# Ten instead of four gate blocks by seven products, six instead of twelve as filler work, and three smaller edits in the attention stage

## The chip, the cores and the metric

One core of a Trainium2 chip runs the kernel. The core has a matrix engine (TensorE, PE in the profile, its weight loads PEld), a vector engine (VectorE, DVE), a scalar engine (ScalarE, ACT), a general engine (GpSimd, POOL) and SyncE (SP), which here issues all DMA transfers. Each engine works its own list of instructions in order, and semaphores make it wait for others. The metric is the device time of one execution in microseconds; lower is better.

## The reference

The input is x, 1024 tokens by 1024 channels, float32. One layer is computed:

```
h = x @ w_in                                   # 1024 x 5120
qa, ka, va, qb, kb, vb, ga, gb = split(h)      # 3 x 512, 3 x 512, 1024, 1024 columns
y_a = chunk_band_attention(qa, ka, va, rel_bias) @ w_proj_a
y_b = stick_breaking_attention(qb, kb, vb) @ w_proj_b
mix = (sigmoid(ga + b) * y_a + sigmoid(gb + b) * y_b) @ w_out
x = layer_norm(alpha * x + mix)
g, u = split(x @ w_ffn_in)                     # 2 x 2816 columns
x = layer_norm(alpha * x + (silu(g) * u) @ w_ffn_out)
```

Each attention has 8 heads of 64 channels. The first (A) is a softmax over a band of nine chunks of 64 tokens with a bias by distance. The second (B) has no softmax: with beta = sigmoid(q.k/8), the weight of an earlier token is its beta times the product of (1 - beta) over all tokens between it and the query.

## The kernel before, in words

All float32 products are made from rounded halves: a value is split into a high part (a cast on ACT) and a low part (a subtraction on DVE, sometimes on POOL), and a product is three matmuls, high by high, high by low and low by high. `split` (lines 105 to 107) and `load_w` (396 to 405) are these splits.

The first stage computes h in blocks of 128 channels by 1024 tokens. The list `work` (line 220 on) names pairs of blocks: query with key, two value blocks, two gate blocks. The first pair is computed plainly (96 matmuls of 512 columns), the others by a scheme of seven instead of eight half-size products (`pair_steps`, 84 matmuls, line 173); the sums of weights that it needs run on DVE and its splits on ACT and DVE. `N_GATE` pairs at the end of the list are gate blocks. Results go to DRAM buffers (`q_dr`, `k_dr`, `v_dr`, `g_dr`) and come back when they are needed.

The attention stage runs 16 heads, first the eight of A, then the eight of B; two heads share one of the eight 128-row result tiles `yt`, which is stored to `y_dr`. A head has eight score blocks of 128 queries ("units", `wunits`) and twelve value steps (`vsteps`; eight for queries 0 to 511, then four for 512 to 1023). The main loop goes step by step. At each step it first issues the score units that are due by the list `LEAD`, some 5 to 13 units ahead and so reaching into the next head; then the step's transposes of the weights (`turn`, line 558), whose results ACT and DVE split; then the value matmuls (`mult`, lines 571 and 572) of the step `LAG` = 2 earlier. Units 2 and 3 of the next head are issued at the steps with numbers 9 and 10 of a head, counted from 0.

A score unit of A (`soft_block`) is: matmuls, a DVE instruction that adds the bias and finds the row minimum of the negated scores (line 494), an exponential on ACT (499), a reciprocal on DVE (501) and a scaling on POOL (502). A unit of B (`stick_block`) is computed in one or two cuts: matmuls, two sigmoids on ACT (527, 528), a running product along the row on DVE (a scan, lines 531 and 535), and a product on POOL (537). In the reversed token order used here a row's running product must start at the diagonal. The first 128 columns of each block hold the diagonal; there the scan multiplies and adds the identity matrix, which starts it with 1. For the other columns the scan multiplies only and takes its start from the column before.

At a group's last value step, ACT copies the value bank (line 578) and DVE adds its upper and lower 64 rows (line 579), since these hold the products with the high and the low part of the values.

Between transposes and value matmuls the loop places filler matmuls, which do not depend on the attention: `fill_all` yields one unit per matmul, and `fill_until` issues units up to a goal. `FILL` gives the units per head of A and of B: 8 x 30 + 8 x 66 = 768 units. They are the gate blocks that are not in `work`, computed plainly (`gate`, 48 matmuls each, line 420), and then projection A (line 608, 192 matmuls), which needs `y_dr[0..3]` back, split into `yh` and `yl` (`reload_y`, lines 629 to 633; the high parts on ACT, the low on POOL). While it runs, `y_dr[4..6]` are brought back too for projection B. The tiles `yh` and `yl` take the places of the input's halves `xh` and `xl`, which the gate blocks read (16 places with the tag `xt`).

After that come projection B (from 684 us), the output projection with the first layer norm, the FFN and the second layer norm. The order of instructions on each engine is the order in which they are traced, except that the planner of the language may issue an instruction earlier when its place and inputs are free in its own estimate; DMA issues in particular move ahead.

Of the kernel before, what the change touches and what calls it, by code (L numbers as in the profile page):

```python
# [14 lines left out]
ALU = mybir.AluOpType  # L15
# [3 lines left out]
P = 128  # L19
# [3 lines left out]
DH = 64  # L23
# [13 lines left out]
LAG = 2  # L37
LEAD = (5, 6, 6, 7, 8, 8, 9, 10, 10, 11, 12, 13)

FILL = (30.0, 66.0)  # L40

# [5 lines left out]
def hybrid_trunk_kernel(ctx: ExitStack, tc, x, xt, w_in, b_gate, rel_bias, w_proj,  # L49
# [6 lines left out]
    nc = tc.nc  # L56
# [170 lines left out]
            if i % 2:  # L227
                work.append(("v", br * 4 + i - 1, br * 12 + 8 + i - 1, br * 12 + 8 + i))

    N_GATE = 2  # L230
    work += [("g", j, 24 + j, 32 + j) for j in range(N_GATE)]
    Wa = [dict() for _ in work]

# [281 lines left out]
    def stick_block(hd, b, be):  # L515

        nm = f"b{hd['n']}_{b}"
        w = (8 - b) * P
        kp = slot("kp", f"kp_{nm}")
        nc.gpsimd.memset(be[:, 0:1], 0.0)  # L520
        c1 = max((4 - b) * P, 320)
        cuts = [(0, c1), (c1, w - c1)] if b < 4 else [(0, w)]
        for c0, n in cuts:
            sc = scores(f"sc_{nm}_{c0}", hd, b, c0, n)
            e = c0 + n
            m0 = max(c0, 1)
            nc.scalar.activation(kp[:, c0:e], sc[:, 0:n], AF.Sigmoid, scale=-1.0)  # L527
            nc.scalar.activation(be[:, m0:e], sc[:, m0 - c0:n], AF.Sigmoid)
            if c0 == 0:

                nc.vector.tensor_tensor_scan(kp[:, 0:P], kp[:, 0:P], ident_ps()[:, 0:P], 0.0,
                                             ALU.mult, ALU.add)
            s0 = max(c0, P)
            if s0 < e:
                nc.vector.tensor_tensor_scan(kp[:, s0:e], kp[:, s0:e], ident_ps()[:, 0:e - s0],  # L535
                                             kp[:, s0 - 1:s0], ALU.mult, ALU.bypass)
            nc.gpsimd.tensor_tensor(be[:, m0:e], be[:, m0:e], kp[:, m0 - 1:e - 1], ALU.mult)  # L537

    def value_steps(hd, g, wt):
# [5 lines left out]
        pv = []  # L545
# [3 lines left out]
        for i, kb in enumerate(kbs):  # L549
# [14 lines left out]
            def mult(i=i, kb=kb, lo_q=lo_q, n=n, pts=pts):  # L564
                v = hd["v"]
                if i == 0:
                    pv.append(bank("pv", f"pv_{nm}"))
                last = i == len(kbs) - 1
                cs = slice((lo_q - q0) * P, (lo_q - q0) * P + n)
                pt = pts[0]  # L570
                mm(pv[0][:, cs], v[:, kb, :], pt[:, 0:n], start=(i == 0), stop=False)
                mm(pv[0][:, cs], v[:, kb, :], pt[:, HW:HW + n], start=False, stop=last)
                if last:
                    yt = hd["yt"]()
                    r = slice(h * DH, (h + 1) * DH)
                    gs = slice(g * HW, (g + 1) * HW)
                    both, cs = (yt, gs) if h == 0 else (slot("yt", f"yv_{nm}"), LO)
                    nc.scalar.copy(both[:, cs], pv[0])
                    nc.vector.tensor_tensor(yt[r, gs], both[0:DH, cs], both[DH:P, cs], ALU.add)
                    if h == 1 and g == 1 and hd["i"] < 7:  # L580
                        dma(y_dr[hd["i"]], yt)

# [4 lines left out]
    def fill_all():  # L587
        w = first_w
        for i in range(first_gate, 16):
            nxt = load_gate(i + 1, nc.gpsimd) if i < 15 else load_proj(0, 0, "op", nc.gpsimd)  # L590
            yield from gate(i, w)
            w = nxt
        for i in range(4):
            reload_y(i, nc.gpsimd)
        for cc in range(4):
            nxt = load_proj(0, cc + 1, "op", nc.gpsimd) if cc < 3 else None
            if cc < 3:
                reload_y(4 + cc, nc.gpsimd)
            for j in range(2):
                c = 2 * cc + j  # L600
                t = slot("gt", f"gA{c}")
# [22 lines left out]
    KEEP, kept = 5, {}  # L624
    yh, yl = [None] * 8, [None] * 8

    def reload_y(i, eng):
        raw = slot("op", f"yraw{i}")
        dma(raw, y_dr[i])
        yh[i] = slot("xt", f"yh{i}", F32R)  # L630
        yl[i] = slot("xt", f"yl{i}", F32R)
        nc.scalar.copy(yh[i], raw)
# [450 lines left out]
```

## Time and profile before

| what | value |
| --- | --- |
| median of three runs | 1477.73 us (1476.61 to 1478.14) |
| the profiled execution | 1479.15 us |
| its span, first to last instruction | 1477.4 us |
| first stage, to the first score matmul | 0 to 291 us |
| attention stage | 291 to 684 us |
| projection B to the end | 684 to 1477 us |

A profile page and the answers drawn from the same trace list groups of instructions by line, engine and operation, with the tiles written and read (`out<-in`), the shapes (partitions x elements), the count, the busy time and the mean duration of one. Then comes the idle time of that engine just before these instructions, and what ended it. The busy time of PE is modelled from pipelined matmuls. A matmul of 512 columns is listed with about 0.39 us, but the next one starts 0.227 us after it.

### The profile page before, as it was taken

How to read it: one execution, taken by the hardware profiler on the slowest of the kernel's cores; microseconds unless marked ns; L12 is line 12 of the kernel's file. 1: busy time of each engine (PE TensorE's matmuls, PEld its weight loads, DVE VectorE, ACT ScalarE, POOL GpSimd, SP SyncE). 2: the span in 40 equal slices, each digit the busy share in tenths (PEclk: the TensorE clock that was granted, in tenths of full speed). 3: DMA queues.
4: the chain of work that ended last, by engine and by line, in shares of the span. 5: the costliest groups of instructions: out<-in, count | busy, mean ns of one | idle time of the engine just before them, and what ended most of it. 6: DMA issues, size and time to landing. Idle time of an engine off the chain costs nothing.

```text
span 1477.4 us, 19005 instructions
## 1 busy us (share of the span) xinstructions
PE 1433.8 (97%) x6728; PEld 1177.4 (80%) x6728; DVE 994.8 (67%) x1633; ACT 679.5 (46%) x1215; POOL 314.5 (21%) x333
## 2 busy tenths in 40 slices
PE   8999999999998999999999899999999999999997
PEld 6788888887787888777788678888888888888886
DVE  8865555276677767786848985555555543885896
ACT  6444444376676656874513443333333332344540
POOL 0000000143336555960003212111111111300021
PEclk9999999999999999999999999999999999999999
DMA  6555544766554355657611133323233335863521
GB/s 214 157 186 171 162 149 158 217 194 175 157 152 135 92 163 188 200 186 242 243 43 58 58 111 125 100 100 105 102 107 103 105 107 207 313 228 93 182 83 72
DMA packets 76176, 219.42 MB, mean 149 GB/s; under 512 B 9504, under 2 KB 9504, under 8 KB 76080
## 3 DMA queue, kind: packets, MB, share of 16 engines
q1 hardware_dynamic: 76080, 218.19, 45.6%
q8 instruction: 53, 0.87, 0.2%
q14 instruction: 43, 0.35, 0.1%
HBM read 149.71 MB, written 68.45 MB: 148 GB/s over the span
## 4 chain that ended last, share of the span: by engine, by line
PE 77%; DVE 9%; DMA 5%; ACT 3%; issue 2%; POOL 2%; SPq 0%; POOLq 0%; DVEq 0%; ACTq 0%
PE sxf L173 15%; PE dn L970 14%; PE sxp L173 9%; PE szf L173 7%; PE gps L420 5%; PE szp L173 5%; PE syf L173 4%; PE syp L173 2%; DVE kp_b L535 2%; PE ops L116 2%; PE ops L114 2%; PE ops L113 2%; PE tp_b L558 2%; PE yAps L608 1%; PE tp_a L558 1%
## 5 line engine op out<-in xcount | busy, mean ns | idle before, releaser
L970 PE MATMUL dn<-dr,dl 128*128 128x512 f32 x924 | 209.6, 389 | 0.0
L970 PEld LDWEIGHTS dn<-dr,dl 128*128 128x128 f32 x924 | 173.4, 188 | 36.1
L537 POOL TENSOR_TENSOR w_b<-w_b,kp_b 128x511 f32<-128x511 f32 (+3 forms) x96 | 99.1, 1036 | 62.2 <-DVE kp_b L535 34.5
L752 POOL TENSOR_TENSOR mv<-mv,neghalf 128x1 f32<-128x1 f32 x16 | 26.9, 1682 | 315.4 <-DVE mv L751 311.4
L106 ACT CAST dl<-raw 128x512 fp32r<-128x512 f32 x77 | 47.5, 623 | 84.8 <-PE dn L970 67.9
L535 DVE TENSOR_TENSOR_SCAN kp_b<-kp_b,ident_ps 128x384 f32<-128x384 f32 (+6 forms) x88 | 78.5, 892 | 4.6
L420 PE MATMUL gps<-xh,wl_g 128*128 128x512 f32 x192 | 80.3, 418 | 0.0
L420 PE MATMUL gps<-xh,wh_g 128*128 128x512 f32 x192 | 80.3, 418 | 0.0
L420 PE MATMUL gps<-xl,wh_g 128*128 128x512 f32 x192 | 80.2, 418 | 0.0
L107 DVE TENSOR_TENSOR dl<-raw,dl 128x512 fp32r<-128x512 f32 x77 | 53.5, 701 | 25.1 <-ACT dl L106 24.7
L527 ACT ACTIVATE kp_b<-sc_b 128x512 f32<-128x512 f32 (+3 forms) x96 | 48.3, 504 | 41.1 <-PE sc_b L464 31.0
L502 POOL TENSOR_SCALAR w_a<-w_a,st_a 128x640 f32<-128x640 f32 (+2 forms) x64 | 46.1, 724 | 82.7 <-DVE st_a L501 69.9
L107 DVE TENSOR_TENSOR pt_b<-tp_b,pt_b 128x512 fp32r<-128x512 f32 (+1 forms) x96 | 51.1, 542 | 18.3 <-ACT pt_b L106 18.2
L481 POOL MEMSET bias<- 64x64 f32 x8 | 1.2, 145 | 275.9 <-ACT bias L480 275.9
L827 POOL TENSOR_TENSOR sb<-h 128x512 f32<-128x512 f32 x10 | 17.8, 1778 | 193.0 <-PE syf L173 97.4
L173 PE MATMUL szf<-x1S63h,wcf 128*128 128x512 f32 x176 | 57.7, 389 | 0.0
L106 ACT CAST pt_b<-tp_b 128x512 fp32r<-128x512 f32 (+1 forms) x96 | 47.8, 498 | 20.8 <-PE tp_b L558 20.3
L106 ACT CAST pt_a<-tp_a 128x512 fp32r<-128x512 f32 (+1 forms) x96 | 40.3, 424 | 27.2 <-PE tp_a L558 26.7
L499 ACT ACTIVATE w_a<-w_a,st_a 128x640 f32<-128x640 f32 (+2 forms) x64 | 44.6, 697 | 17.4 <-DVE st_a L494 16.6
L558 PE MATMUL tp_b<-ident,w_b 128*128 128x128 f32 x288 | 48.3, 275 | 4.2 <-DVE pt_b L107 1.8
L186 DVE TENSOR_TENSOR gt<-sxf,gt 128x512 f32<-128x512 f32 x22 | 15.1, 688 | 54.6 <-PE sxf L173 54.6
L107 DVE TENSOR_TENSOR pt_a<-tp_a,pt_a 128x512 fp32r<-128x512 f32 (+1 forms) x96 | 45.6, 485 | 8.2 <-ACT pt_a L106 8.1
(1541 smaller groups left out, 4218.9 us busy)
## 6 DMA issues: line engine op xcount, KB each, us to landing
raw<-left_dr SPq DMA_DIRECT2D x77, 256.0 KB, 3.0
wLf<-in_w_ffn_in_dram SPq DMA_DIRECT2D x22, 512.0 KB, 3.9
wRf<-in_w_ffn_in_dram SPq DMA_DIRECT2D x22, 512.0 KB, 4.2
rows<-in_w_ffn_out_dram SPq DMA_DIRECT2D x22, 512.0 KB, 6.1
left_dr<-h SPq DMA_DIRECT2D x33, 256.0 KB, 2.0
v_dr<-v SPq DMA_DIRECT2D x16, 512.0 KB, 3.6
kl<-k_dr SPq DMA_DIRECT2D x32, 256.0 KB, 6.4
v<-v_dr SPq DMA_DIRECT2D x16, 512.0 KB, 3.3
```

The source lines that it names most:

```text
L106: nc.scalar.copy(dst_h, src)
L107: nc.vector.tensor_tensor(dst_l, src, dst_h.bitcast(F32), ALU.subtract)
L113: mm(acc, lh, rh, start=(i == 0), stop=False)
L173: mm(acc, lw[:, ks], rx, start=(first and kt == i == 0), stop=(kt == 3 and i == 2), skip_group_check=not first)
L420: mm(acc, lw[:, ks], rx[k][:, cs], start=(k == j == 0), stop=(k == KT - 1 and j == 2))
L499: nc.scalar.activation(s[:, 0:w], s[:, 0:w], AF.Exp, bias=st[:, m:m + 1], scale=-1.0, accum_out=st[:, 2:3])
L502: nc.gpsimd.tensor_scalar(s[:, 0:w], s[:, 0:w], st[:, 3:4], 0.0, ALU.mult, ALU.add)
L527: nc.scalar.activation(kp[:, c0:e], sc[:, 0:n], AF.Sigmoid, scale=-1.0)
L535: nc.vector.tensor_tensor_scan(kp[:, s0:e], kp[:, s0:e], ident_ps()[:, 0:e - s0], kp[:, s0 - 1:s0], ALU.mult, ALU.bypass)
L537: nc.gpsimd.tensor_tensor(be[:, m0:e], be[:, m0:e], kp[:, m0 - 1:e - 1], ALU.mult)
L558: tr(tp[:, (qb - lo_q) * P:(qb - lo_q + 1) * P], wt[qb - q0][:, (kb - qb) * P:(kb - qb + 1) * P], ident)
L970: mm(acc, lw, rx, start=(fresh and steps[s][1] == n == 0), stop=(last and n == 2), skip_group_check=not fresh)
```

## The change

Four things change.

- `N_GATE` goes from 2 to 5: five gate pairs (ten blocks) are in the first stage's list, and the fillers start with block 10, so six plain gate blocks remain. `FILL` goes to (18, 42): 8 x 18 + 8 x 42 = 480 units.
- In `stick_block` each cut has a single scan. A first cut multiplies and adds the identity's columns followed by zeros over its whole width; a second cut multiplies only, as before.
- The copies of both value groups go side by side into one 1024-wide tile, and one addition of 64 x 1024 is made after the second group. For the last tile (i = 7) the additions stay at 512.
- `reload_y` becomes `load_y` (the DMA) and `split_y` (the halves). For the first four tiles the loads are traced at filler units 6, 12, 18 and 26 of the last gate block, the splits at its units 28, 34, 40 and 46, instead of after it. Tiles 4 to 6 follow one pass of projection A later than before.

```diff
-FILL = (30.0, 66.0)
+FILL = (18.0, 42.0)
...
-    N_GATE = 2
+    N_GATE = 5
...
-            if c0 == 0:
-
-                nc.vector.tensor_tensor_scan(kp[:, 0:P], kp[:, 0:P], ident_ps()[:, 0:P], 0.0,
-                                             ALU.mult, ALU.add)
-            s0 = max(c0, P)
-            if s0 < e:
-                nc.vector.tensor_tensor_scan(kp[:, s0:e], kp[:, s0:e], ident_ps()[:, 0:e - s0],
-                                             kp[:, s0 - 1:s0], ALU.mult, ALU.bypass)
+            nc.vector.tensor_tensor_scan(kp[:, c0:e], kp[:, c0:e], ident_ps()[:, 0:n],
+                                         kp[:, c0 - 1:c0] if c0 else 0.0,
+                                         ALU.mult, ALU.bypass if c0 else ALU.add)
...
-                    both, cs = (yt, gs) if h == 0 else (slot("yt", f"yv_{nm}"), LO)
-                    nc.scalar.copy(both[:, cs], pv[0])
-                    nc.vector.tensor_tensor(yt[r, gs], both[0:DH, cs], both[DH:P, cs], ALU.add)
+                    if h == 1 and "yv" not in hd:
+                        hd["yv"] = slot("yt", f"yv_{nm}")
+                    both = hd.get("yv", yt)
+                    nc.scalar.copy(both[:, gs], pv[0])
+                    if hd["i"] == 7:
+                        nc.vector.tensor_tensor(yt[r, gs], both[0:DH, gs], both[DH:P, gs], ALU.add)
+                    elif g == 1:
+                        nc.vector.tensor_tensor(yt[r], both[0:DH], both[DH:P], ALU.add)
...
-            yield from gate(i, w)
+            for n, unit in enumerate(gate(i, w)):
+                if i == 15:
+                    if n in (6, 12, 18, 26):
+                        load_y((6, 12, 18, 26).index(n))
+                    if n in (28, 34, 40, 46):
+                        split_y((28, 34, 40, 46).index(n), nc.gpsimd)
+                yield unit
             w = nxt
-        for i in range(4):
-            reload_y(i, nc.gpsimd)
         for cc in range(4):
             nxt = load_proj(0, cc + 1, "op", nc.gpsimd) if cc < 3 else None
-            if cc < 3:
-                reload_y(4 + cc, nc.gpsimd)
+            if cc:
+                load_y(3 + cc)
+                split_y(3 + cc, nc.gpsimd)
...
-    def reload_y(i, eng):
-        raw = slot("op", f"yraw{i}")
-        dma(raw, y_dr[i])
+    yraw = {}
+
+    def load_y(i):
+        yraw[i] = slot("op", f"yraw{i}")
+        dma(yraw[i], y_dr[i])
+
+    def split_y(i, eng):
+        raw = yraw.pop(i)
         yh[i] = slot("xt", f"yh{i}", F32R)
         yl[i] = slot("xt", f"yl{i}", F32R)
         nc.scalar.copy(yh[i], raw)
```

## The prediction

> **What bounds the kernel now.** I read the page first, then busy time by stretches cut at the stages, then who waited for whom inside the attention stage, then single heads in order of time.
>
> ```profile
> span 1477.4 us, 19005 instructions
> PE 1433.8 (97%) x6728; PEld 1177.4 (80%) x6728; DVE 994.8 (67%) x1633; ACT 679.5 (46%) x1215; POOL 314.5 (21%) x333
> PE 77%; DVE 9%; DMA 5%; ACT 3%; issue 2%; POOL 2%; SPq 0%; POOLq 0%; DVEq 0%; ACTq 0%
> ```
>
> PE sets the pace over the whole span; only in places does something else. The change touches the first stage (to 290.9 us) and the attention stage (290.9 to 684.3). The next rows are busy times by stretch: the last seven-product pair of the first stage, then heads 0, 1 to 6, 7 (with the scores of head 8), 8 to 11, 12, 13, 14 and 15. Heads 0 to 7 are softmax (A), 8 to 15 stick-breaking (B). I cut them where the last value matmul of a head starts.
>
> ```profile
> 255.60:274.64 19.04, 19.04 (x85) 15.76 (x85) 4.85 (x6) 5.94 (x8) 0.58 (x4) 1.00 0.61 188
> 290.90:315.80 24.90, 23.96 (x141) 19.62 (x139) 18.63 (x70) 18.45 (x46) 12.32 (x16) 1.00 0.68 181
> 315.80:433.20 117.40, 112.05 (x650) 93.35 (x649) 81.50 (x276) 77.91 (x196) 45.07 (x60) 1.00 0.57 166
> 433.20:457.50 24.30, 20.89 (x117) 16.85 (x115) 20.11 (x41) 18.32 (x44) 15.12 (x24) 1.00 0.42 111
> 457.50:572.50 115.00, 112.98 (x602) 94.23 (x601) 83.61 (x132) 73.65 (x169) 63.02 (x85) 1.00 0.46 137
> 572.50:601.00 28.50, 28.32 (x152) 23.62 (x151) 20.24 (x33) 20.22 (x43) 17.21 (x22) 1.00 0.63 207
> 601.00:633.10 32.10, 29.05 (x152) 23.37 (x151) 25.15 (x39) 25.44 (x51) 27.80 (x28) 1.00 0.74 224
> 633.10:663.20 30.10, 29.17 (x153) 23.42 (x151) 24.48 (x41) 21.56 (x45) 17.96 (x19) 1.00 0.53 189
> 663.20:684.30 21.10, 21.10 (x115) 17.70 (x114) 12.92 (x23) 12.28 (x23) 2.21 (x3) 1.00 0.50 164
> ```
>
> The columns are length, then busy time and count of PE, PEld, DVE, ACT and POOL, the granted clock, DMA share and GB/s. A pair takes 19.04 us for 84 matmuls, so a 512-wide matmul costs 0.2267 us. An A head takes 117.40/6 = 19.57 us, of which PE idles (117.40 - 112.05)/6 = 0.89; a B head takes 115.00/4 = 28.75 and idles 0.5. DVE needs 13.6 and 20.9 us of these. PE has the longer list only because of the filler matmuls, and the change takes 40% of these away. What the other engines then do to PE is the whole question.
>
> **The change part by part.** *Six gates move.* Three pairs come into the first stage, six plain gates of 48 matmuls leave the fillers.
>
> First stage: 3 x 19.04 = +57.1 us. The row above shows such a pair at full PE with DVE busy 4.85, ACT 5.94 and DMA at 0.61, so its weight sums, splits, two loads and two stores lie under PE at no cost; if that cover went, the sums and splits of a pair would have 14 us of DVE time left.
>
> Attention: 288 x 0.2267 = -65.3 us if every filler taken out is time taken out. Net -8.2. From ACT and POOL go also these casts and splits, twelve gate copies, six weight loads and six stores of SP's queue:
>
> ```profile
> L404 POOL TENSOR_TENSOR wl_g<-wr_g,wh_g 128x1024 fp32r<-128x1024 f32 x11 | 27.2, 2477 | 15.5 <-PE sxp L173 13.0 <-issue 1.2 <-PE gps L420 1.2
> L403 ACT CAST wh_g<-wr_g 128x1024 fp32r<-128x1024 f32 x12 | 12.6, 1051 | 12.4 <-DMA wr_g<-in_w_in_dram 11.2 <-POOL w_b L537 1.2
> ```
>
> That is 15 us of POOL and 6 of ACT, off the path.
>
> *Waits that grow.* Fillers are spread over twelve steps a head: 2.5 a step become 1.5 in A, 5.5 become 3.5 in B. A chain that has k steps to finish loses k x 0.227 us of cover in A and k x 0.453 in B. The tightest is unit 3, the fourth score block of the next head: its scores are issued two steps before the head's first transposes need it. In A (head 6), in order of time, with the waits of heads 0 to 7 below:
>
> ```profile
> 407.39 0.41 PE L463 MATMUL sc_a<-kh,qs 128*128 128x320 f32 x1
> 408.54 0.69 DVE L579 TENSOR_TENSOR yt<-yv_a 64x512 f32<-64x512 f32 x1
> 409.26 0.49 DVE L494 CUSTOM_DVE_ANT_0 w_a<-sc_a,bias 128x320 f32<-128x320 f32 x1
> 412.20 1.47 POOL L502 TENSOR_SCALAR w_a<-w_a,st_a 128x640 f32<-128x640 f32 x2 [1.40 <-DVE st_a L501]
> 413.05 0.33 PE L558 MATMUL tp_a<-ident,w_a 128*128 128x128 f32 x1 [0.31 <-POOL w_a L502]
> ...
> PEld sc_a L463 <- DVE st_a L494: 6.0, 18, 0.8
> PEld tp_a L558 <- POOL w_a L502: 5.3, 8, 1.2
> PEld pv_a L571 <- ACT yt L578: 3.9, 4, 2.3
> 406.60:411.40 4.80, 4.65 (x26) 3.57 (x25) 4.52 (x16) 2.82 (x7) 1.10 (x2) 1.00 0.01 3
> ```
>
> PE already waits at the head's start, so the two steps' 0.45 us would be pure loss. But the value add of 0.69 us stands between the scores and their reduction on DVE, and the change moves it to the head's end. So 0.45 - 0.69 = -0.24; I take 0, between -0.24 and +0.45. The wait for the copy of the value bank loses 1.5 fillers, 0.34; I take 0.2. The score banks' 18 waits (2.3 a head) could each grow by 0.23, 0.5 in all; I take 0.1, because DVE, 94% busy in the last row, loses the same 0.69 there. A head: +0.3 (-0.24 to 1.3); seven heads +2.1 (-1.7 to 9.1). Head 7 has DVE at 20.11 of 24.30 and about 14 fillers (3.1 us) fewer, while DVE loses an add and four scan starts; +1.0 (0 to 2).
>
> *One scan per first block.* 64 first scans of 128 columns go, 56 of the 88 following ones grow by 128 columns:
>
> ```profile
> L531 DVE TENSOR_TENSOR_SCAN kp_b<-kp_b,ident_ps 128x128 f32<-128x128 f32 x64 | 26.6, 416 | 30.1 <-ACT kp_b L527 27.6 <-ACT w_b L528 2.0
> L535 DVE TENSOR_TENSOR_SCAN kp_b<-kp_b,ident_ps 128x512 f32<-128x512 f32 x16 | 20.5, 1279 | 1.5
> L535 DVE TENSOR_TENSOR_SCAN kp_b<-kp_b,ident_ps 128x384 f32<-128x384 f32 x16 | 16.2, 1014 | 0.5
> L535 DVE TENSOR_TENSOR_SCAN kp_b<-kp_b,ident_ps 128x192 f32<-128x192 f32 x16 | 9.8, 613 | 0.5
> ```
>
> (1279 - 613)/320 = 2.08 ns a column, 213 ns fixed; 128 columns should then take 480, and the adding form takes 416, so it is no slower. A merged scan of 512 takes 1.22 to 1.28 us where 0.42 + 1.01 stand, which saves 0.15 to 0.21. If its second operation cost more per column (416 ns all columns: 3.25 ns), 512 would take 1.66 and lose 0.23; I take 0.18 saved, seven a head, 1.3 us of DVE.
>
> *Value rows.* Seven pairs of B and A heads trade two adds for one:
>
> ```profile
> L579 DVE TENSOR_TENSOR yt<-yt 64x512 f32<-64x512 f32 x16 | 16.5, 1031 | 2.1 <-ACT yt L578 1.6
> L404 DVE TENSOR_TENSOR wl_o<-wr_o,wh_o 128x1024 fp32r<-128x1024 f32 x8 | 9.7, 1218 | 0.9 <-ACT wh_o L403 0.9
> 527.00:541.40 14.40, 13.87 (x74) 11.31 (x73) 13.54 (x21) 10.92 (x27) 9.56 (x10) 1.00 0.36 105
> 541.40:555.80 14.40, 14.40 (x79) 12.11 (x78) 8.27 (x15) 8.04 (x19) 5.37 (x12) 1.00 0.46 133
> ```
>
> A 1024-wide add should take 1.22 undisturbed, up to 2 x 1.03. What matters is where: a B head's second six steps (first of the two stretches) keep DVE 94% busy, the other six 57%, and the early add leaves the full half for the other. In the full half, twelve fillers go: 14.40 - 2.72 = 11.7 us of PE against 13.54 - 1.03 - 4 x 0.18 = 11.8 of DVE. The late stretch's rest spills into the light half as it does now. On unit 3's chain in B the slack now is:
>
> ```profile
> 509.27 1.60 DVE L535 TENSOR_TENSOR_SCAN kp_b<-kp_b,ident_ps 128x192 f32<-128x192 f32 x2
> 510.03 0.87 POOL L537 TENSOR_TENSOR w_b<-w_b,kp_b 128x319 f32<-128x319 f32 x1 [1.80 <-DVE kp_b L535]
> 511.33 0.63 PE L558 MATMUL tp_b<-ident,w_b 128*128 128x128 f32 x4 [0.18 <-DVE pt_b L107]
> ```
>
> POOL ends at 510.90, the fourth transpose starts about 511.66: 0.76 us. Two steps take 0.91 away, the merged scan and the moved add give 0.2 to 1.2 back. I take +0.5 a head for the fuller DVE, heads 8 to 11: +2.0 (-2.0, all their idle time gone, to 4.8, the 0.91 and 0.3 beside it).
>
> The Trainium skill (SBUF — State Buffer, SBUF: two separate sides) says that a DVE instruction with two SBUF inputs and a GpSimd one that reads SBUF exclude each other for a whole instruction. By it, one 1.22 us add would hold POOL once where two of 0.69 held it twice, 0.16 less in all but 0.53 longer in one piece; put on every head's path it would add 14 x 0.53 = 7 us to the sum. The trace agrees in so far as that add takes 1.03 on average and 0.69 in the row at 408.54, with no POOL row beside it.
>
> *Projection A's operands.* The loads now stand in the last gate, the splits in its second half. What they can win is this:
>
> ```profile
> 591.18 2.39 POOL L633 TENSOR_TENSOR yl<-yraw,yh 128x1024 fp32r<-128x1024 f32 x1
> 597.93 2.41 POOL L633 TENSOR_TENSOR yl<-yraw,yh 128x1024 fp32r<-128x1024 f32 x1
> PE yAps L608 <- POOL yl L633: 2.6, 2, 1.4
> ```
>
> PE waits 2.6 us for the splits in head 13, whose POOL is busy 27.8 of 32.1 us. Afterwards the last half gate lasts 24/3.5 = 6.9 steps instead of 4.4, for four splits of 2.4 us between POOL's products. No queue is held: ACT and POOL wait for a matmul at most one filler ahead. I take -2.0 for heads 13 and 14 (-3.0 to +1.0). Head 12 becomes a projection head with its 3.5 gated products a head on DVE: +1.0 (0 to 2). Head 15, where little DVE work is left, +0.5 (0 to 1).
>
> *Sum.* +57.1 - 65.3 + 2.1 + 1.0 + 2.0 + 1.0 - 2.0 + 0.5 = -3.6; with all ends low -14.9, all high +11.7. The profiled execution took 1479.15 us (1.75 around its span), 1.42 above the median of 1477.73. So 1475.6 against that execution, 1474 for the median.
>
> **The rivals.** *The chains take over (slower).* Place: unit 3 at every head's start. If neither moved add nor merged scan shortens it because splits and sigmoids ahead of it fill the gap, A heads lose 0.9 (0.45, 0.34 and 0.1), B heads 1.0: 7 x 0.9 + 2 + 4 x 1.0 + 1.5 (heads 12 to 15) = +13.8, so +5.6 and 1483. For: A's chain has no slack, DVE is at 94% in both critical stretches. Against: both edits cut just there. It decides from 8.2 us of new waiting, half a microsecond a head.
>
> *The DVE edits free more.* If they also end the idle time of heads 8 to 14 and the banks' waits in A, the extras are -4: 1466. For: 2.0 + 3.05 + 0.93 us idle stand in those rows. Against: fewer fillers hide less.
>
> *The operand move does nothing.* The first split already runs at 591.18, before the last gate ends at 599, so the order on POOL may hardly change: 2 us less, 1476.
>
> *The clock drops.* With fewer 512-wide matmuls PE might be granted half speed, as it was after this hole:
>
> ```profile
> 846.00:850.00 4.00, 1.23 (x3) 0.48 (x3) 4.00 (x6) 1.67 (x2) 0.00 (x0) 1.00 0.00 0
> 850.00:854.00 4.00, 2.05 (x5) 1.66 (x6) 3.76 (x6) 3.12 (x4) 0.00 (x0) 0.50 0.33 110
> ```
>
> Such a spell of 4 us costs 2; one in every second head would be +16: 1490. Against it: an A head keeps 112.05/6 - 2.72 = 16.0 us of PE in some 17, where the first row shows PE 31% busy. The Trainium skill (TensorE: Matmul & The Clock Gate, Why this matters for your kernels) wants no idle gaps over about 3 us, which agrees.
>
> **How the numbers follow.** Forecast 0.43 (its own range 1470 to 1478), chains 0.27, more freed 0.20, idle operand move 0.08, clock 0.02. A measurement of this kernel tells 0.2%, 3.0 us, from no change. Faster: 0.20 and a little over half of the forecast, 0.45. Slower: the chains and the clock, nearly all, 0.28. The rest, 0.27, is within. The range 1464 to 1484 reaches from the freed case to the chains.
>
> **What would show it.** First stage ending near 348 us; 288 gate fillers in three rows of 96; A heads near 17.1 us, heads 8 to 11 near 23.8; no scan of 128 beside a second one in a first block, 512 columns at 1.2 us; 1024-wide adds near 1.2 us; hardly a wait of the projection for a split. Wrong would make it: A heads above 17.6 with the transposes waiting for POOL, or B heads above 24.5 with DVE over 90%; for the other side, B heads under 23.

## The result and the profile after

The changed kernel took 1470.42 us (median of six, 1468.46 to 1472.87), the kernel before 1477.93 in the same call: a ratio of 0.9949 [0.9937, 0.9961], 7.5 us less. The forecast was 3.6 less. The execution with the profile was the slowest of the six, 1472.87 us, so the two profiles differ by 6.3 us where the medians differ by 7.5. Its mean granted clock was 0.992 and that of the other five 0.994 to 0.996, so the others ran less at half clock; how much of the two spells below they share isn't known.

The page after, its span and its busy times:

```profile
span 1471.1 us, 18930 instructions
PE 1428.4 (97%) x6692; PEld 1174.6 (80%) x6692; DVE 1002.0 (68%) x1596; ACT 681.4 (46%) x1221; POOL 300.5 (20%) x327
```

Nothing can be read there: PE's share is what it was. Busy times by stretch, cut as in the prediction (heads 0, 1 to 6, 7, 8 to 10, 11, 12, 13, 14, 15), then short stretches inside heads 12 and 15 (the last 3.41 us before each spell of half clock, and the spells themselves), then projection B:

```profile
347.80:369.80 22.00, 21.19 (x126) 17.43 (x124) 16.56 (x66) 17.24 (x42) 10.35 (x14) 1.00 0.78 204
369.80:471.40 101.60, 96.39 (x580) 80.75 (x578) 79.90 (x273) 74.85 (x195) 45.61 (x60) 1.00 0.59 171
471.40:491.10 19.70, 17.77 (x103) 14.40 (x102) 16.89 (x33) 16.43 (x42) 14.06 (x24) 1.00 0.49 148
491.10:559.40 68.30, 68.18 (x381) 57.08 (x379) 56.58 (x77) 52.53 (x125) 43.14 (x63) 1.00 0.60 174
559.40:583.70 24.30, 23.13 (x128) 19.09 (x127) 21.16 (x28) 22.65 (x47) 24.30 (x25) 1.00 0.63 195
583.70:611.30 27.60, 24.97 (x129) 20.23 (x127) 22.39 (x29) 20.41 (x44) 19.77 (x25) 0.94 0.68 210
611.30:634.30 23.00, 22.71 (x129) 19.09 (x127) 20.66 (x30) 17.76 (x41) 13.70 (x21) 1.00 0.60 183
634.30:658.60 24.30, 22.98 (x128) 18.78 (x127) 21.96 (x31) 18.44 (x42) 15.56 (x18) 1.00 0.46 160
658.60:679.50 20.90, 18.08 (x95) 15.03 (x94) 12.05 (x22) 12.98 (x23) 2.88 (x4) 0.93 0.49 174
587.76:591.17 3.41, 1.53 (x10) 1.26 (x10) 3.38 (x4) 1.04 (x2) 0.87 (x2) 1.00 1.02 300
673.09:676.50 3.41, 0.92 (x6) 0.43 (x4) 0.77 (x3) 3.10 (x5) 0.00 (x0) 1.00 0.12 50
591.20:594.60 3.40, 3.40 (x11) 2.70 (x10) 1.90 (x4) 1.48 (x5) 1.32 (x5) 0.50 0.91 296
676.50:679.90 3.40, 3.40 (x11) 3.02 (x12) 1.94 (x5) 1.42 (x3) 0.00 (x0) 0.50 0.35 72
679.50:724.70 45.20, 45.04 (x195) 35.93 (x195) 37.43 (x54) 21.31 (x28) 0.00 (x0) 1.00 0.79 276
```

Projection B before, for the last row:

```profile
684.30:731.60 47.30, 45.05 (x196) 35.84 (x195) 37.87 (x54) 21.89 (x29) 0.00 (x0) 1.00 0.80 275
```

The account by stage, profile against profile:

- First stage: 347.8 - 290.9 = +56.9 (forecast +57.1).
- Attention: 331.7 (347.8 to 679.5) against 393.4, -61.7. Of that -65.3 are the fillers, so the extra waits are +3.6 (forecast +4.6).
- After the attention: 791.6 against 793.1, -1.5 (forecast nothing). Projection B is 2.1 shorter, and 0.6 is given back later.
- Sum -6.3.

The sum of the waits was nearly right. Its parts were not. A part is how much PE's idle time (length less busy) changes from the prediction's rows to these, plus half of the time at half clock:

| heads | idle before | idle after | at half clock | extra | forecast |
|---|---|---|---|---|---|
| 0 to 6 | 0.94 + 5.35 | 0.81 + 5.21 | - | -0.3 | +2.1 |
| 7 | 3.41 | 1.93 | - | -1.5 | +1.0 |
| 8 to 11 | 2.02 | 0.12 + 1.17 | - | -0.7 | +2.0 |
| 12 | 0.18 | 2.63 | +1.70 | +4.2 | +1.0 |
| 13, 14 | 3.05 + 0.93 | 0.29 + 1.32 | - | -2.4 | -2.0 |
| 15 | 0 | 2.82 | +1.50 | +4.3 | +0.5 |

Heads 8 to 10 are the surprise: 0.12 us of idle PE in 68.30, with DVE busy 83% of the time. Heads 12 and 15 are the other one, on the opposite side.

Two groups of DVE work after, by line and shape (busy in all and mean ns of one behind the first bar): the merged scans and the wide adds.

```profile
L529 DVE TENSOR_TENSOR_SCAN kp_b<-kp_b,ident_ps 128x512 f32<-128x512 f32 x32 | 40.0, 1249 | 12.1 <-ACT kp_b L527 8.8 <-POOL yl L643 1.5
L579 DVE TENSOR_TENSOR yt<-yt 64x1024 f32<-64x1024 f32 x7 | 13.0, 1859 | 1.1 <-ACT yt L575 1.1
L579 DVE TENSOR_TENSOR yt<-yv_b 64x1024 f32<-64x1024 f32 x3 | 7.1, 2361 | 0.8 <-ACT yv_b L575 0.7
L579 DVE TENSOR_TENSOR yt<-yv_a 64x1024 f32<-64x1024 f32 x4 | 5.3, 1324 | 0.5 <-ACT yv_a L575 0.5
```

The 32 scans of 512 are 16 of the old following kind (1279 ns) and 16 merged ones, which so take 2 x 1249 - 1279 = 1219 ns if the old kind still takes what it took: the bottom of the forecast 1.22 to 1.28. The merged scan of 384 columns takes 947 ns where 416 + 747 stood. An add of 1024 takes from 1.32 to 2.36 us on average.

### The profile page after: what moved, and what is told of

Read it like the earlier page. It is cut to its first block, busy times and chain, and to the rows that moved or that the text cites. A ratio compares the mean times of both kernels' runs of the same rounds, so it can differ in the third digit from the quotient of the medians.

```text
span 1471.1 us, 18930 instructions
## 1 busy us (share of the span) xinstructions
PE 1428.4 (97%) x6692; PEld 1174.6 (80%) x6692; DVE 1002.0 (68%) x1596; ACT 681.4 (46%) x1221; POOL 300.5 (20%) x327
## 4 chain that ended last, share of the span: by engine, by line
PE 49%; DVE 3%; DMA 1%; POOL 1%; ACT 0%; issue 0%; POOLq 0%; DVEq 0%; SPq 0%; ACTq 0%
PE sxf L173 15%; PE dn L980 14%; PE szf L173 8%; PE syf L173 4%; PE ops L116 2%; PE ops L114 2%; PE ops L113 2%; PE yBps L113 1%; PE yBps L114 1%; PE yBps L116 1%; DMA gB<-g_dr 1%; DVE bn L759 0%; DMA wLf<-in_w_ffn_in_dram 0%; DVE x1S57l L107 0%; DVE acc L763 0%
## 5 line engine op out<-in xcount | busy, mean ns | idle before, releaser
L529 DVE TENSOR_TENSOR_SCAN kp_b<-kp_b,ident_ps 128x512 f32<-128x512 f32 (+3 forms) x96 | 92.9, 968 | 17.0 <-ACT kp_b L527 11.7
L107 DVE TENSOR_TENSOR dl<-raw,dl 128x512 fp32r<-128x512 f32 x77 | 54.4, 712 | 25.4 <-ACT dl L106 24.9
L502 POOL TENSOR_SCALAR w_a<-w_a,st_a 128x640 f32<-128x640 f32 (+2 forms) x64 | 49.9, 782 | 65.5 <-DVE st_a L501 50.6
L186 DVE TENSOR_TENSOR c<-sxp,c 128x512 f32<-128x512 f32 x16 | 11.1, 691 | 74.3 <-issue 41.2
L527 ACT ACTIVATE kp_b<-sc_b 128x512 f32<-128x512 f32 (+3 forms) x96 | 50.7, 528 | 23.5 <-PE sc_b L464 22.3
L528 ACT ACTIVATE w_b<-sc_b 128x511 f32<-128x511 f32 (+3 forms) x96 | 51.0, 531 | 0.0
L113 PE MATMUL ops<-wh_o,mh 128*128 128x512 f32 x128 | 50.2, 392 | 0.0
L116 PE MATMUL ops<-wh_o,ml 128*128 128x512 f32 x128 | 50.0, 391 | 0.0
L114 PE MATMUL ops<-wl_o,mh 128*128 128x512 f32 x128 | 49.9, 390 | 0.0
```

The costliest lines, as they stand in the source:

```text
L107: nc.vector.tensor_tensor(dst_l, src, dst_h.bitcast(F32), ALU.subtract)
L113: mm(acc, lh, rh, start=(i == 0), stop=False)
L114: mm(acc, lh, rl, start=False, stop=False)
L116: mm(acc, ll, rh, start=False, stop=(i == n))
L502: nc.gpsimd.tensor_scalar(s[:, 0:w], s[:, 0:w], st[:, 3:4], 0.0, ALU.mult, ALU.add)
L529: nc.vector.tensor_tensor_scan(kp[:, c0:e], kp[:, c0:e], ident_ps()[:, 0:n], kp[:, c0 - 1:c0] if c0 else 0.0, ALU.mult, ALU.bypass if c0 e ...
```

## The experiments

Each edit is shown against the changed kernel, or against the kernel before where that is said. Ratios are to the kernel before, with their 95% intervals, from five rounds; 0.0010 is 1.5 us. All of these kernels compute the whole output.

### The gates alone, and the edits alone

First only the gates and their goals, on the kernel before. With the shorter list the result tiles 4 to 6 would come back before head 13 has written one of them, so they come back one pass later, as in the changed kernel:

```
-FILL = (30.0, 66.0)
+FILL = (18.0, 42.0)
...
-    N_GATE = 2
+    N_GATE = 5
...
-            if cc < 3:
-                reload_y(4 + cc, nc.gpsimd)
+            if cc:
+                reload_y(3 + cc, nc.gpsimd)
```

> Kernel before with ten gates by seven products and the smaller filler goals alone (the reloads of tiles 4 to 6 one pass later, which the shorter filler list needs); old scans, old value adds, old place of the other reloads. Cover theory (fewer fillers hide less; the DVE edits keep the waits from growing): -8.2 us of matmuls, about +7 to +10 of new waits at unit 3 of each head and in DVE-bound stretches: 1477 to 1480 us. Count theory (only the number of matmuls matters, the small edits lie beside it): 1470 to 1472 us.

Measured: 1488.28 us, 1.0067 [1.0053, 1.0081]. By itself the gate move, the first thing in the title of the change, costs 10 us, more than either theory had. Heads 1 to 6 and heads 8 to 10 of this kernel:

```profile
371.40:470.70 99.30, 95.14 (x576) 80.09 (x575) 79.86 (x278) 74.10 (x193) 39.02 (x59) 1.00 0.61 175
492.00:568.70 76.70, 70.62 (x379) 58.01 (x379) 63.99 (x102) 53.05 (x124) 42.87 (x63) 0.98 0.50 153
```

Who waited for whom in these heads 8 to 10 (us in all, times, longest):

```profile
PEld tp_b L558 <- POOL w_b L537: 7.0, 4, 2.4
PE tp_b L558 <- DVE pt_b L107: 5.7, 3, 2.0
```

The A heads lose nothing: 16.55 us a head, their idle time 0.69 a head where it was 0.89. The B heads lose: 25.57 each, and PE's transposes wait for POOL's products and DVE's splits. PE also runs at half clock for 3.41 us here (from 540.0 us), behind such waits. The same waits of the changed kernel's heads 8 to 10 come to this:

```profile
PEld tp_b L553 <- DVE pt_b L107: 0.7, 3, 0.4
```

Then the three small edits without the gates:

```
-FILL = (18.0, 42.0)
+FILL = (30.0, 66.0)
...
-    N_GATE = 5
+    N_GATE = 2
```

> Changed kernel with N_GATE 2 and the old filler goals: the three small edits alone. Cover theory: the long filler list already hides DVE, so only head 13's wait for the operands can go: 1476 to 1477.5 us. If the small edits carry a good part of the gain by themselves: 1474 us or less. Count theory: no change, 1477.9 us.

Measured: 1471.98 us, 0.9959 [0.9944, 0.9974]. The edits alone have four fifths of the gain of the whole change (0.9949); the difference, 1.5 us, lies inside the intervals. So the gates lose 10 us without the edits. With them a gain of 1.5 is measured that isn't told apart from none. The edits gain about 6 us at the old goals and 17 at the new.

### Which edit: the scans, the wide add

The old two scans put back in the changed kernel:

```
-            nc.vector.tensor_tensor_scan(kp[:, c0:e], kp[:, c0:e], ident_ps()[:, 0:n],
-                                         kp[:, c0 - 1:c0] if c0 else 0.0,
-                                         ALU.mult, ALU.bypass if c0 else ALU.add)
+            if c0 == 0:
+                nc.vector.tensor_tensor_scan(kp[:, 0:P], kp[:, 0:P], ident_ps()[:, 0:P], 0.0,
+                                             ALU.mult, ALU.add)
+            s0 = max(c0, P)
+            if s0 < e:
+                nc.vector.tensor_tensor_scan(kp[:, s0:e], kp[:, s0:e], ident_ps()[:, 0:e - s0],
+                                             kp[:, s0 - 1:s0], ALU.mult, ALU.bypass)
```

> Changed kernel with the two scans per first cut put back. Cover theory: 1.3 us more of DVE in each B head at 81 to 90% DVE, about 0.7 a head lost: 1474 to 1476 us, B heads 8 to 10 at 23.3 us or more instead of 22.8. Count theory: 1470.5 us, heads unchanged.

Measured: 1473.65 us, 0.9968 [0.9957, 0.9980]: 2.8 us less gained than by the change, with intervals that overlap a little.

The old two adds put back, each at its own group's end:

```
-                    if h == 1 and "yv" not in hd:
-                        hd["yv"] = slot("yt", f"yv_{nm}")
-                    both = hd.get("yv", yt)
-                    nc.scalar.copy(both[:, gs], pv[0])
-                    if hd["i"] == 7:
-                        nc.vector.tensor_tensor(yt[r, gs], both[0:DH, gs], both[DH:P, gs], ALU.add)
-                    elif g == 1:
-                        nc.vector.tensor_tensor(yt[r], both[0:DH], both[DH:P], ALU.add)
+                    both, cs = (yt, gs) if h == 0 else (slot("yt", f"yv_{nm}"), LO)
+                    nc.scalar.copy(both[:, cs], pv[0])
+                    nc.vector.tensor_tensor(yt[r, gs], both[0:DH, cs], both[DH:P, cs], ALU.add)
```

> Changed kernel with the two 512-wide value adds put back. Cover theory: the add stands in unit 3's chain again, 0.3 to 0.5 a head lost, less the long locked adds of heads 5, 11 and 12 (2 to 3 us in all): 1472 to 1474 us. Count theory: 1470.5 us. If the 1024-wide add locked out by POOL costs more than the chain gains: 1468 to 1469 us.

Measured: 1479.22 us, 1.0000 [0.9989, 1.0012]. Without the wide add the change gains nothing; that is more than any of the theories gave the add. Heads 8 to 10 with the old scans:

```profile
492.30:562.60 70.30, 68.79 (x380) 56.46 (x377) 59.93 (x98) 52.42 (x123) 42.91 (x63) 1.00 0.57 168
```

and, with the old adds, heads 1 to 6 and 8 to 10:

```profile
370.30:469.70 99.40, 95.23 (x576) 80.20 (x576) 79.95 (x278) 74.17 (x193) 39.02 (x59) 1.00 0.61 175
490.50:562.20 71.70, 67.98 (x379) 56.89 (x377) 59.56 (x80) 52.56 (x124) 42.28 (x62) 1.00 0.54 162
```

Put the rows of heads 8 to 10 beside the changed kernel (68.30 us, DVE busy 56.58) and the gates alone (76.70 and 63.99): in all four DVE is busy 83 to 85% of the stretch, where it was 73% at the old goals (83.61 of 115.00). PE's work is nearly the same in them but for the half clock, and what differs is its idle time: 0.12 us in the changed kernel, 1.51 with the old scans, 3.72 with the old adds, 6.08 with the gates alone, which have both. It goes up as DVE gets more to do, though not by the amount alone: the old adds bring less DVE work than the old scans and more idle time. So the changed kernel's heads 8 to 10 are still paced by PE (68.18 of 68.30 us), and it takes little more work on DVE for the chains behind it to hold PE up. The old scans add 3.35 us of DVE work and 2.0 us of time in these three heads.

The wide add alone, on the kernel before (the edit of the last diff, reversed):

> Kernel before with the wide value add alone (12 filler gates, old scans, old reloads). If the place of the add is also what gives the three edits their 6 us at the old filler goals: 1473 to 1475 us. If the scans or the reloads give that gain: 1477 to 1478 us.

Measured: 1472.01 us, 0.9957 [0.9943, 0.9971], all that the three edits together gain at the old goals. Its heads 8 to 11 and, beside it, those of the kernel with the three edits:

```profile
454.00:566.90 112.90, 112.30 (x603) 94.50 (x602) 80.77 (x130) 73.61 (x169) 63.09 (x85) 1.00 0.46 141
```

```profile
454.10:567.00 112.90, 112.27 (x604) 94.85 (x603) 75.81 (x101) 73.83 (x169) 62.92 (x85) 1.00 0.46 140
```

The scans take another 5 us off DVE and the length stays where it is: with the wide add in place 5 us of DVE's work no longer count at the old goals, and PE is idle for 0.6 of 112.9 us. At the new goals the same scans are worth 2.8 us, by intervals that overlap.

### Is it the add's place or its width?

The wide add differs from the old two in two ways: the first half is added later, and one instruction does both. Two adds of 512 at the place of the wide one:

```
-                        nc.vector.tensor_tensor(yt[r], both[0:DH], both[DH:P], ALU.add)
+                        for c2 in (LO, HI):
+                            nc.vector.tensor_tensor(yt[r, c2], both[0:DH, c2], both[DH:P, c2], ALU.add)
```

> Changed kernel with the value rows added by two instructions of 512, but both at the end of the head as the wide one is. Place theory (what gained 8 us over the old adds is that DVE's full second half of a head lost one of them): 1470 to 1472 us, B heads 8 to 10 near 22.9 us. Width theory (one instruction instead of two is what pays): 1475 us or more, heads near 23.9 us as with the old adds.

Measured: 1480.91 us, 1.0010 [0.9996, 1.0025], no gain. But this kernel didn't do what it was made for. In order of time in head 8:

```profile
509.22 1.38 DVE L580 TENSOR_TENSOR yt<-yt 64x512 f32<-64x512 f32 x1
517.37 1.24 DVE L580 TENSOR_TENSOR yt<-yt 64x512 f32<-64x512 f32 x1 [0.29 <-ACT yt L575]
```

The two adds stand next to each other in the program and 8 us apart on the engine: the planner puts the first one back to where its input is ready. So the run says nothing of width. It was made again with both adds held behind the last split traced before them:

```
+                        with tc.issue_after(last_split[0]):
+                            for c2 in (LO, HI):
+                                nc.vector.tensor_tensor(yt[r, c2], both[0:DH, c2], both[DH:P, c2],
+                                                        ALU.add)
```

> Changed kernel with two value adds of 512, both held on DVE behind the split traced last before the head's end, because in the run before the planner put the first of the two back to its old early place (389.56, 509.22, 533.05 us and so on). Place theory: now the early half of the adds is out of DVE's full stretch, heads 8 to 10 at 22.6 to 23.1 us, 1470 to 1473 us. Width theory (one instruction instead of two is what pays): heads 8 to 10 at 23.8 us as in the run before, 1478 us or more.

Measured: 1473.48 us, 0.9972 [0.9957, 0.9987]; heads 8 to 10:

```profile
492.30:561.70 69.40, 68.41 (x380) 57.23 (x379) 57.84 (x80) 52.60 (x125) 42.95 (x63) 1.00 0.59 171
```

With the place alone the ratio falls from 1.0010 to 0.9972, 5.6 us, and that lies outside the intervals. One instruction in place of two brings 0.9949, another 3.4 us; here the intervals overlap a little, so this part isn't settled by the times. The wide instruction is also what keeps the planner from pulling the first half forward: it can't start before the second half is there.

### The operand move

The old order, all reloads after the last gate (tiles 4 to 6 still one pass later):

```
-            for n, unit in enumerate(gate(i, w)):
-                if i == 15:
-                    if n in (6, 12, 18, 26):
-                        load_y((6, 12, 18, 26).index(n))
-                    if n in (28, 34, 40, 46):
-                        split_y((28, 34, 40, 46).index(n), nc.gpsimd)
-                yield unit
+            yield from gate(i, w)
...
+        for i in range(4):
+            reload_y(i, nc.gpsimd)
```

> Changed kernel with the first four tiles reloaded and split after the last gate, as before (tiles 4 to 6 still one pass later). If the new place did the work: PE waits 2 to 3 us again for the low parts, 1472.5 to 1473.5 us. If the planner had hoisted the splits anyway: 1470 to 1471 us, the first low part still computed before the last gate ends.

Measured: 1472.04 us, 0.9951 [0.9935, 0.9968], the same as the whole change. POOL's first split here, and then in the changed kernel:

```profile
556.19 2.39 POOL L633 TENSOR_TENSOR yl<-yraw,yh 128x1024 fp32r<-128x1024 f32 x1
```

```profile
556.90 2.40 POOL L643 TENSOR_TENSOR yl<-yraw,yh 128x1024 fp32r<-128x1024 f32 x1
```

It runs at the same place. The planner moves the splits ahead by itself, and the hand-written order adds nothing to it. Two earlier kernels show what took away the projection's wait for the splits, 2.6 us before. With the edits alone, hand-written order and old goals, it is still there:

```profile
PE yAps L613 <- POOL yl L643: 2.3, 2, 1.4
```

With the gates alone, old order and new goals, no such wait is listed, and none in the changed kernel. So it goes with the goals and not with the order.

### Two more gates

Six pairs of gates in the first stage, four plain gates as fillers:

```
-FILL = (18.0, 42.0)
+FILL = (14.0, 34.0)
...
-    N_GATE = 5
+    N_GATE = 6
```

> Changed kernel with twelve gates by seven products (N_GATE 6) and four plain ones, FILL (14, 34). Count theory: another -2.7 us, 1467.7 us. Cover theory: 16 fillers more are lost in heads 1 to 8 and again in 8 to 15, with DVE at 80 to 90% of a head the waits grow by 0.2 to 0.5 a head: 1469 to 1473 us, A heads' idle PE time up by 0.3 or more, B heads above 90% DVE.

Measured: 1471.61 us, 0.9952 [0.9933, 0.9970], no further gain. Heads 1 to 6, heads 8 to 10, and head 10 by itself:

```profile
387.60:481.10 93.50, 90.76 (x553) 75.96 (x552) 77.82 (x273) 73.16 (x192) 40.88 (x60) 1.00 0.66 187
500.30:567.70 67.40, 64.08 (x353) 51.64 (x351) 56.65 (x78) 56.71 (x128) 50.64 (x67) 1.00 0.62 188
543.89:567.60 23.71, 21.61 (x120) 17.47 (x119) 19.81 (x27) 22.32 (x46) 22.48 (x25) 1.00 0.64 200
```

The time is what the cover theory had, but its signs didn't come: the A heads still shrink, by 1.35 us each, and idle 0.46 each, less than the changed kernel's 0.87; DVE in heads 8 to 10 is at 84%. There PE loses 4.1 us of work and the time falls by 0.9. Most of the new idle time, 2.1 of 3.3 us, lies in head 10, where splits for the projection now run: ACT and POOL are busy 22.3 and 22.5 of its 23.7 us. So these rows don't show that DVE sets a floor here.

### Head 12

In head 12 of the changed kernel, in order of time:

```profile
583.95 2.31 POOL L532 TENSOR_TENSOR w_b<-w_b,kp_b 128x511 f32<-128x511 f32 x2
585.85 3.85 DVE L579 TENSOR_TENSOR yt<-yv_b 64x1024 f32<-64x1024 f32 x1 [0.74 <-ACT yv_b L575]
586.16 2.46 POOL L643 TENSOR_TENSOR yl<-yraw,yh 128x1024 fp32r<-128x1024 f32 x1
590.48 0.66 PE L553 MATMUL tp_b<-ident,w_b 128*128 128x128 f32 x4 [1.88 <-DVE pt_b L107]
```

The add takes 3.85 us in place of the 1.22 that it takes with no POOL row beside it (316.74 us of the kernel with the edits alone). It begins while the second of the two products runs, and it ends at 589.70, 1.08 after POOL's split, so it waited for that split as well. The split of the weights that stands behind it on DVE is late, PE waits 1.88 us, and the half clock from 591.2 follows. One head earlier the same kind of meeting went another way:

```profile
560.93 3.06 DVE L579 TENSOR_TENSOR yt<-yt 64x1024 f32<-64x1024 f32 x1
562.86 2.00 POOL L532 TENSOR_TENSOR w_b<-w_b,kp_b 128x383 f32<-128x383 f32 x1
```

Here the add begins during a split that ends at 562.91, and it ends at 563.99, 1.08 later, while POOL's next product is under way and takes 2.00 us where one of 383 columns took 1.01 elsewhere (565.08 us of the next kernel). The add got in between two POOL instructions. If the length of POOL's instructions is the cause, halves of 512 should let the add in earlier:

```
+        for cs in (LO, HI):
+            eng.tensor_tensor(yl[i][:, cs], raw[:, cs], yh[i][:, cs].bitcast(F32), ALU.subtract)
```

(and the same for the weight splits on POOL)

> Changed kernel with each 1024-wide split on POOL done as two of 512. Lock theory (a value add waits for whole POOL instructions that read two SBUF tiles): the adds of 2.98, 3.06 and 3.85 us fall to 2.5 or less, PE's 2.0 us wait in head 12 shrinks to about 1: 1468.5 to 1469.5 us. If the adds are long for another reason they stay, and the time stays 1470.5 us or grows by POOL's extra starts.

Measured: 1472.25 us, 0.9955 [0.9938, 0.9973], no difference to the change. In head 5 the add falls from 2.98 to 1.88 us and in head 11 from 3.06 to 2.08, as the lock theory had it. In head 12 it doesn't. Rows of heads 11 and 12:

```profile
561.59 3.54 POOL L645 TENSOR_TENSOR yl<-yraw,yh 128x512 fp32r<-128x512 f32 x2
561.89 2.08 DVE L580 TENSOR_TENSOR yt<-yt 64x1024 f32<-64x1024 f32 x1
585.75 2.29 POOL L533 TENSOR_TENSOR w_b<-w_b,kp_b 128x511 f32<-128x511 f32 x2
587.24 4.35 DVE L580 TENSOR_TENSOR yt<-yv_b 64x1024 f32<-64x1024 f32 x1 [0.72 <-ACT yv_b L576]
587.97 2.55 POOL L645 TENSOR_TENSOR yl<-yraw,yh 128x512 fp32r<-128x512 f32 x2
592.38 0.66 PE L554 MATMUL tp_b<-ident,w_b 128*128 128x128 f32 x4 [2.38 <-DVE pt_b L107]
```

In head 11 the add ends between the two halves' ends. In head 12 it begins during the second product, takes 4.35 us and ends 1.07 after the second half, so it waited out both halves, and PE waits 2.38 us. So one long split is the cause in heads 5 and 11, and not in head 12. Why the add comes last only there isn't shown.

### Head 15

In head 15, in order of time:

```profile
669.61 1.15 ACT L648 ACTIVATE gB<-gB,bg 128x1024 f32<-128x1024 f32 x1 [2.08 <-DMA gB<-g_dr]
...
675.86 0.57 ACT L575 COPY yv_b<-pv_b 128x512 f32<-128x512 f32 x1
676.48 0.80 PE L566 MATMUL pv_b<-pt_b,v 128*128 128x512 f32 x1 [2.49 <-ACT yv_b L575]
```

The sigmoids of projection B's gates have been issued early, ahead of the value bank's copy, and hold ACT's queue while their DMA is under way. PE waits 2.49 us for the copy behind them. Here they are held behind that copy (`last_free[0]`):

```
+        if br == 0:
+            nc.scalar.activation(t, t, AF.Sigmoid, bias=bg[:, col:col + 1])
+        else:
+            with tc.issue_after(last_free[0]):
+                nc.scalar.activation(t, t, AF.Sigmoid, bias=bg[:, col:col + 1])
```

> Changed kernel with projection B's sigmoids held on ACT behind the first value copy of the last head. If ACT, waiting for the gate DMA ahead of that copy, is what holds PE 2.5 us in head 15: 1467.5 to 1468.5 us. If those sigmoids only move that wait to the start of projection B: 1470 to 1471 us.

Measured: 1469.53 us, 0.9936 [0.9917, 0.9955], the fastest kernel of this study, though not told apart from the change by its interval, and 1 us above the range of the theory that named the cause. Head 15 is 3.2 us shorter, at full clock, and no wait of PE for that copy is left. The second row is projection B:

```profile
657.90:675.60 17.70, 17.37 (x98) 14.48 (x98) 12.43 (x21) 10.96 (x22) 2.85 (x4) 1.00 0.59 211
675.58:720.47 44.89, 43.78 (x192) 35.36 (x191) 36.54 (x52) 23.37 (x30) 0.00 (x0) 1.00 0.77 275
```

It takes 44.9 us, so it doesn't need the early sigmoids to be shorter than the 47.3 before.

On this kernel POOL's splits were then held behind the stick-breaking product traced last before them (`last_pool[0]`), so that none is pulled ahead of it into head 12's meeting:

```
+        with tc.issue_after(last_pool[0]):
+            eng.tensor_tensor(yl[i], raw, yh[i].bitcast(F32), ALU.subtract)
```

> Changed kernel with projection B's sigmoids held back as in the run before, and POOL's splits of the reloaded tiles held behind the stick-breaking product traced last before them, so that the planner cannot put them earlier. If head 12 is long because its 1024-wide add meets a hoisted split on POOL: no add there above 2.5 us, head 12 at 25.5 us or less instead of 27.5, 1466.5 to 1468 us. If head 12 is long because DVE and POOL have more to do there than PE: head 12 at 27 us, 1469 to 1470 us.

Measured: 1474.36 us, 0.9971 [0.9959, 0.9982], worse. Its head 12, and the value add and a sigmoid in it:

```profile
585.80:614.90 29.10, 25.30 (x129) 19.94 (x127) 20.36 (x29) 20.29 (x44) 18.58 (x24) 0.94 0.62 199
587.87 1.70 DVE L586 TENSOR_TENSOR yt<-yv_b 64x1024 f32<-64x1024 f32 x1 [0.74 <-ACT yv_b L580]
596.34 1.15 ACT L657 ACTIVATE gA<-gA,bg 128x1024 f32<-128x1024 f32 x1 [4.63 <-DMA gA<-g_dr]
```

The edit did what it was made for, the add takes 1.70 us, and yet the head takes 29.1 us where the change has 27.6. Now ACT stands 4.63 us at a sigmoid of projection A's gates whose transfer is under way, PE waits 2.4 us for ACT, and a spell of half clock follows: the fault of head 15, in head 12. So the meeting of the add with POOL's split explains the wait in the row at 590.48, and that it explains the head's length isn't shown. With the old scans, where the add in head 12 takes 1.22 us, that head takes 26.0 us at full clock; the changed kernel's 27.6 us hold 1.7 us of half clock. What head 12 would take with neither the meeting nor ACT's stop stays open.

## Why the prediction was right, and where it was wrong

*The first stage (+57.1).* Right: +56.9. A seven-product pair costs what the quoted pair costs, and its sums, splits and transfers stay under PE.

*The fillers (-65.3).* Right. The attention stage is 61.7 us shorter, PE's idle time and half clock in it grow by 3.6, and the difference of the two is this number.

*A heads (+2.1).* Wrong by 2.4 us, and for the wrong reason. The step said that two steps' cover would be a pure loss, and that the moved value add would give it back. The gates alone, with the add in its old place, idle less in heads 1 to 6 than the kernel before, 0.69 a head where it was 0.89; with the old adds in the changed kernel (the row at 370.30) it is 0.70; with the wide add 0.87. So the loss wasn't there to be made up. What the step left out isn't shown; it took the whole of the lost cover as new waiting and let nothing else move.

*Heads 8 to 11 (+2.0).* Wrong by 2.7 us: -0.7. The step saw the place rightly (the full half of a B head, 11.8 us of DVE against 11.7 of PE) and took 0.5 a head for it. But heads 8 to 10 got rid of nearly all their idle time, which the prediction had as the low end of that term. The first rival, chains that take over, is what happens without the edits: +9.9 us in the run of the gates alone where the rival had +5.6, most of it in the B heads (25.57 each in heads 8 to 10, where 28.75 less 24 fillers would be 23.31). The edits that I priced at fractions of a microsecond a head decide the sign here. The scans took 0.21 off each pair (forecast 0.18), and that was right.

*The wide add.* The prediction said "What matters is where", and the run with two held adds bears that out: the place is worth 5.6 us of the change. But it gave the add no term of its own. At the old goals, where my steps name no chain that needs it, it alone gains 0.0043, about 6 us. How it does that in the A heads isn't settled: they are 2.3 us shorter with it (115.1 for six against 117.4) at the old goals, and 2.2 longer (101.60 against 99.40) at the new, 0.9 of which are four matmul records more.

*The lock.* The rows first: the fourteen wide adds take 25.4 us together, where 14 x 1.22 = 17.1 would be undisturbed, 8.3 more. Before the change the 32 adds of 512 took 16.5 + 8.3 + 6.2 = 31.0, where 32 x 0.69 = 22.1 would be undisturbed, 8.9 more, so in all the change added no such time. In the prediction I estimated 7 us by the Trainium skill (SBUF — State Buffer, SBUF: two separate sides); that this is near 8.3 is chance, since my 7 us were POOL held longer by the adds, and the 8.3 are adds held by POOL. The 0.53 us that the estimate rests on does show on POOL: a product of 383 columns behind a wide add in head 9 takes 2.01 us (516.29), behind the add of 512 in the kernel with the old adds 1.47 (516.83). Much of it costs PE nothing: in heads 8 to 10 the three adds take 1.62 to 1.78 us, and PE idles 0.12 us in all. (I read the 1.03 us of one group of adds as the mean of the add at 408.54; that one belongs to another group, with 0.77.)

*Heads 13 and 14 (-2.0).* -2.4, the right number by luck, from the wrong step. The order of loads and splits written into the last gate was not what did it: without it the time is the same. The rival that the move does nothing was right about the mechanism. The projection's wait for the splits goes with the new goals. That this is the whole gain of these two heads isn't shown: with the gates alone they idle 4.9 us for other reasons.

*Head 12 (+1.0) and head 15 (+0.5).* Both wrong by more than 3 us in the profile, 1.7 and 1.5 of which are half clock. For head 12 the step counted DVE's work. It had neither the add's meeting with POOL's split, behind which 1.88 us of the idle time stand, nor the clock; how much of the 4.2 us the meeting causes stays open. For head 15 it looked at DVE, where there is room, and not at ACT's queue: the sigmoids of projection B aren't part of the change, and I didn't ask what is issued earlier when the fillers end earlier. That is shown by the run that holds them back. The 2.1 us that projection B is shorter aren't given back by them, since it is as short in that run. Before the change PE waited 2.0 us there for DVE's products with the gates, and 0.2 after; why isn't shown.

*The clock (0.02).* It came true in a small way: two spells of 3.4 us at half clock, 3.2 us in all, both behind waits in these two heads. With the gates alone a spell came in heads 8 to 10 too, behind the waits that the missing fillers uncovered, so the rival's way to half clock exists; the edits closed it there.

So the time fell inside the range, on the side that was called, and twice as far down as forecast. The parts that were too high (A heads, heads 7 to 11) and those too low (12 and 15) nearly cancel in the profile, +3.6 against +4.6, and that they do is luck. The rest of the difference is projection B and the medians. The forecast also had the gain come from the gates, -8.2, with the edits only holding down its price. Measured, the wide add alone gains about 6 us with no gate moved, and the gates on top of the edits gain 1.5, inside the intervals.

## What to carry to other kernels

Where filler work hides chains, ask before taking it away which engine needs the larger share of that stretch next: here the same change of goals lost 10 us with DVE's old work, and lost nothing with 7 us less of it in three heads. A small instruction on a chain can be worth more by its place than by its length, and a planner that moves instructions ahead by its own estimate undoes a late place unless the instruction's inputs force it. After any change that ends a stage earlier, look at what each in-order engine now issues early, and at the transfer that it then stands waiting for.

## What the runs showed of the hardware

A DVE add with two SBUF inputs, 64 x 1024, that begins while POOL runs an instruction with two SBUF inputs ends 1.08 us after it: 3.06 us in head 11 and 1.78 in head 9 of the changed kernel, 1.22 with nothing beside it. The POOL instruction queued behind then takes 2.00 us where 1.01 stood. The Trainium skill (SBUF — State Buffer, SBUF: two separate sides) has the lock go by whole instructions to whichever starts first, and these rows agree. In head 12 the add waited out the next instruction too (3.85 us, and 4.35 with two half splits); why isn't shown.

PE fell to half clock for 3.41 us after waits of 1.88 and 2.49 us. In the 3.41 us before, it was busy 1.53 and 0.92 us (the rows at 587.76 and 673.09). All four spells in this trace begin a whole number of steps of 3.413 us apart (25, 73 and 256 steps after the first, at 676.50, 840.34 and 1464.98 us). In the kernel with half splits PE waits 2.38 us, from 590.00 to 592.38, and keeps full clock; laid from that kernel's own spells, the border of two steps falls at 591.78, inside the wait, and in the step before it PE is busy 1.63 of 3.41 us. So the length of one wait alone doesn't decide. These rows fit the busy share of such a step, but that isn't settled either: the first kernel with two late adds keeps full clock after a step with 1.51 us busy (598.54 to 601.95).

The Trainium skill (TensorE: Matmul & The Clock Gate, Why this matters for your kernels) asks for no idle gaps over about 3 us; here half clock followed waits of 1.88 and 2.49 us.
